# Attention scores as two 64-row matmuls side by side instead of one 128-row matmul over zero-padded queries

## The chip, the cores and the metric

The kernel runs on all eight cores of one Trainium2 chip (two dies, cores 0 to 3 and 4 to 7). Every core does the same program on its own data; no core waits for another. The metric is the device time in microseconds of the slowest core. A run can fall into a slower state, in which the cores of one die or both show a lower granted clock of TensorE (one run of control before: 2176.61 us, with 0.86 to 0.87 on cores 0 to 3 and 0.998 to 0.999 on the others, against 1933.28 us with 0.997 to 0.999 on all); such runs are left out wherever times are compared: a time given for several runs is the median of the fast ones.

"TensorE" is PE in the profile, "ScalarE" is ACT, "VectorE" is DVE, "GpSimd" is POOL.

## The reference, cut to what matters

One step of a two-layer encoder: gated linear attention (GLA), an FFN, forgetting attention (Fox), an FFN. A core has one prompt stream of 2048 tokens and four sample streams of 64 tokens with 2048 cached keys each. Only Fox changes here. It has 16 heads of 64 columns:

```python
def fox_attend(q, k, v, c_q, c_k, q_pos, k_pos):
    s = jnp.einsum('bqhd,bkhd->bhqk', q, k).astype(jnp.float32) * (FOX_HD ** -0.5)   # FOX_HD = 64
    bias = c_q.transpose(0, 2, 1)[:, :, :, None] - c_k.transpose(0, 2, 1)[:, :, None, :]
    mask = k_pos[None, :] <= q_pos[:, None]
    p = jax.nn.softmax(jnp.where(mask, s + bias, MASK_VALUE), axis=-1)
    return jnp.einsum('bqhk,bkhd->bqhd', p.astype(v.dtype), v)
# cut: projections, cumulative log-forget gates, GLA, SwiGLU FFN, RMSNorm, caches
```

## The kernel before

The kernel describes its work as nodes (a group of matmuls, an exp, a copy, a transfer). A list scheduler in Python, with a cost model of its own, fixes the order on each engine before the kernel is built; one helper emits everything, so that every instruction carries that helper's line (L566 before, L568 after). A table of seeded random changes of priority, `SHUFFLE`, was found by search against the cost model. It is tuning for one exact list of nodes.

Two heads share the 128 rows of a tile. The score matmul contracts over all 128 rows at once: the queries are stored block-diagonally, half of the buffer zero, and 512 columns (two heads by 256 queries) come out into one PSUM bank.

```python
Q = U.ring("a_q", 3, [128, 2, 2, 256], BF16)      # zeroed once; half of it stays zero
BS = Banks([0, 1, 2])                             # scores: three single banks
BO, BOS = Banks([3, 4]), Banks([5])               # outputs of prompt, of samples
BP = Banks([6, 7, 0, 1, 2])                       # projections; shares banks with the scores

def a_item(p, tt, hf, a):                         # one key block of 128 for 256 queries of two heads
    # cut
    b = BS.next()
    pt = PT.next()
    g.mm([(bank(b, 2 * w), kT[:, a * 128:(a + 1) * 128], q[:, hf, :, c0:256], True, True)], ...)
    # cut: causal mask on the diagonal
    g.act(pt[:, 0:2 * w], bank(b, 2 * w), AF.Exp, [pk(b)], [(pt.name,)], scale=0.125)
    if a == 0:
        obk[0] = BO.next()
    ob = obk[0]
    g.mm([(bank(ob, 65, ...), pt[:, ...128 columns], vt[:, a, h, :], ...) for h in range(2) for qt in range(c0 // 128, 2)], ...)

def s_item(p, s, gq):                             # samples: four cached key blocks
    b = BS.next()
    g.mm([(bank(b, 128, c0=j * 128), kc[:, ...], qb[:, s, :, :], True, True) for j in range(4)], ...)
    # cut: exp of 512 columns, four matmuls with the values
```

The softmax here doesn't subtract the row's maximum and nothing guards it: scores larger than these inputs give would overflow.

## Time and profile before

| | before |
|---|---|
| time | 1943.97 us, median of 3 runs (1942.37 to 1950.3); the profiled execution was a faster one |
| TensorE busy in the profiled run | 98% of 1931.9 us |
| Fox stage, ScalarE / VectorE / GpSimd busy | about 72% / 63% / 54% |
| granted clock of TensorE | 0.998 |

The first lines show parts 1, 3 and 4 of the page of the kernel before (its slowest core): busy us, share of the span and count of instructions for each engine; a DMA queue's packets, MB and share; the chain that ended last, by engine.

```profile
span 1931.9 us, 39044 instructions; the slowest of 8 cores (1920.0 to 1931.9 us)
...
PE 1885.6 (98%) x14130; PEld 1094.1 (57%) x14130; DVE 914.6 (47%) x1783; ACT 886.1 (46%) x1580; POOL 484.5 (25%) x573
...
q8 instruction: 118, 1.93, 0.4%
...
PE 90%; DVE 3%; issue 2%; ACT 2%; DMA 1%; POOL 1%; SPq 0%; ACTq 0%; DVEq 0%; POOLq 0%
...
```

TensorE is the limit: it is busy nearly all the time, and the chain of waits that ended last is 90% its work.

The table by stage of the same run, in three stretches of Fox (columns: stretch, its length, busy us and instructions of each engine, granted clock, share of the DMA engines, GB/s):

```profile
...
895.00:1060.00 165.00, 163.30 (x1996) 114.86 (x1994) 95.50 (x232) 121.84 (x233) 110.42 (x136) 1.00 0.76 171
1060.00:1240.00 180.00, 175.69 (x2125) 122.83 (x2123) 109.86 (x268) 129.40 (x249) 114.12 (x141) 1.00 0.74 162
1240.00:1450.00 210.00, 206.00 (x2074) 129.28 (x2072) 144.62 (x326) 146.95 (x272) 77.32 (x93) 1.00 0.46 99
...
```

No other engine is near its limit, and TensorE has 10 us of gaps in 555. The costliest exps of ScalarE on the page (out and in, count, busy us, mean ns, idle before it and what ended it):

```profile
...
L566 ACT ACTIVATE a_P_264<-ps 128x512 bf16<-128x512 f32 x96 | 57.5, 599 | 25.9 <-PE ps L566 15.5
...
L566 PE MATMUL ps<-a_q_258,a_kT_243 128*128 128x512 bf16 (+1 forms) x108 | 35.8, 366 | 0.0
...
```

An exp of 512 columns takes 0.6 us. A record of a matmul lasts 378 ns (366 on average with the narrow ones), but the next matmul starts before it ends, so what a matmul costs is the distance from its start to the next start: 216 ns for 512 columns over 128 rows, 109 ns for 256, 56 ns for 128.

### The profile page before, as it was taken

Reading aid. Unit: us, or ns where it says so; the run is one execution under the profiler, and the core shown is the slowest. Engines: PE = TensorE matmul, PEld = TensorE weight load, DVE = VectorE, ACT = ScalarE, POOL = GpSimd, SP = SyncE. Lnnn points to the kernel's source line nnn. Section 1 sums busy time; section 2 is a strip of 40 time slices with the busy share of each in tenths; the row PEclk is TensorE's granted clock in tenths of the full one; section 3 lists DMA queues with packets and bytes.
Section 4 is the critical chain, followed back from the end, with each engine's and each line's share of the span. In section 5 each row is a group of like instructions: output and inputs, shape, how many; then the busy total and the mean of one; then the engine's idle time right before and its main releaser. Section 6 shows DMA issues by size and latency. Waiting matters only on the chain.

```text
span 1931.9 us, 39044 instructions; the slowest of 8 cores (1920.0 to 1931.9 us)
## 1 busy us (share of the span) xinstructions
PE 1885.6 (98%) x14130; PEld 1094.1 (57%) x14130; DVE 914.6 (47%) x1783; ACT 886.1 (46%) x1580; POOL 484.5 (25%) x573
## 2 busy tenths in 40 slices
PE   6999999999999999999999999999999999999998
PEld 3545655455555444486776676766555555544447
DVE  3877677532111622246457566577855121162225
ACT  5776788531100611113777677776754110051112
POOL 2431111300000000017665665663213000000000
PEclk9999999999999999999999999999999999999999
DMA  9604402343244533327876876775225323495222
GB/s 187 158 8 66 103 1 47 61 74 59 45 68 80 96 67 63 62 41 174 184 170 149 169 163 140 178 163 112 56 43 90 60 45 60 82 189 108 46 45 89
DMA packets 84027, 183.69 MB, mean 95 GB/s; under 512 B 6912, under 2 KB 17024, under 8 KB 83840
## 3 DMA queue, kind: packets, MB, share of 16 engines
q0 software_dynamic: 37488, 103.88, 32.5%
q1 hardware_dynamic: 46352, 77.31, 14.2%
q8 instruction: 118, 1.93, 0.4%
q14 instruction: 69, 0.57, 0.1%
HBM read 253.96 MB, written 31.08 MB: 148 GB/s over the span
## 4 chain that ended last, share of the span: by engine, by line
PE 90%; DVE 3%; issue 2%; ACT 2%; DMA 1%; POOL 1%; SPq 0%; ACTq 0%; DVEq 0%; POOLq 0%
PE ps L566 90%; DMA gsp_out<-g_SF_111 1%; DMA x<-xin 0%; DVE x L566 0%; POOL g_rs_107 L566 0%; POOL f_rs_131 L566 0%; DVE h_3_316 L566 0%; ACT g_re_85 L566 0%; DVE h_1_142 L566 0%; DVE h_0_114 L566 0%; ACT g_Sb_84 L566 0%; ACT L566 0%; DMA g_St_125<-state_in 0%; DVE h_1_148 L566 0%; DVE h_3_306 L566 0%
## 5 line engine op out<-in xcount | busy, mean ns | idle before, releaser
L566 DVE TENSOR_TENSOR x<-ps,x 128x512 f32<-128x512 f32 (+2 forms) x344 | 200.5, 600 | 241.6 <-PE ps L566 239.3
L566 ACT ACTIVATE f_sg_300<-ps 128x512 bf16<-128x512 f32 (+1 forms) x46 | 25.8, 560 | 162.2 <-PE ps L566 147.3
L566 ACT ACT_TABLE_LOAD x45 | 57.7, 1283 | 33.7 <-PE ps L566 18.0
L566 ACT ACTIVATE a_P_264<-ps 128x512 bf16<-128x512 f32 x96 | 57.5, 599 | 25.9 <-PE ps L566 15.5
L566 DVE TENSOR_TENSOR ps<-ps,a_neg 128x256 f32<-128x256 f32 x128 | 53.2, 426 | 33.3 <-PE ps L566 32.2
L566 ACT ACTIVATE a_P_266<-ps 128x512 bf16<-128x512 f32 x96 | 57.2, 596 | 24.0 <-PE ps L566 14.6
L566 ACT ACTIVATE f_sq_190<-x 128x512 bf16<-128x512 f32 (+1 forms) x12 | 10.1, 841 | 123.9 <-PE ps L566 100.8
L566 ACT ACTIVATE a_P_262<-ps 128x512 bf16<-128x512 f32 x96 | 57.4, 598 | 19.2 <-PE ps L566 14.9
L566 ACT ACTIVATE f_sg_128<-ps 128x512 bf16<-128x512 f32 (+1 forms) x33 | 17.3, 526 | 97.1 <-PE ps L566 97.1
L566 ACT ACTIVATE a_P_265<-ps 128x512 bf16<-128x512 f32 (+1 forms) x96 | 53.2, 554 | 13.4 <-PE ps L566 10.1
L566 ACT ACTIVATE f_sq_302<-x 128x1024 bf16<-128x1024 f32 (+2 forms) x24 | 20.2, 843 | 83.3 <-DVE x L566 73.8
L566 ACT ACTIVATE a_P_263<-ps 128x512 bf16<-128x512 f32 (+1 forms) x96 | 53.5, 557 | 10.1 <-PE ps L566 7.8
L566 PE MATMUL ps<-a_oT_250,a_wo_268 128*128 128x512 bf16 (+1 forms) x160 | 56.9, 357 | 0.7 <-DVE x L566 0.5
L566 ACT ACTIVATE a_P_267<-ps 128x512 bf16<-128x512 f32 (+1 forms) x96 | 51.6, 537 | 11.8 <-PE ps L566 8.8
L566 PE MATMUL ps<-a_oT_299,a_wo_268 128*128 128x512 bf16 (+1 forms) x160 | 56.9, 357 | 0.0
L566 ACT ACTIVATE f_sq_303<-x 128x1024 bf16<-128x1024 f32 (+2 forms) x24 | 20.1, 840 | 79.9 <-DVE x L566 76.2
L566 ACT ACTIVATE f_sg_189<-ps 128x512 bf16<-128x512 f32 x22 | 13.1, 596 | 80.3 <-PE ps L566 78.0
L566 ACT ACTIVATE f_sg_301<-ps 128x512 bf16<-128x512 f32 (+1 forms) x46 | 25.7, 559 | 36.4 <-PE ps L566 36.4
L566 PE MATMUL ps<-a_q_258,a_kT_243 128*128 128x512 bf16 (+1 forms) x108 | 35.8, 366 | 0.0
L566 PE MATMUL ps<-a_q_258,a_kT_291 128*128 128x512 bf16 (+1 forms) x102 | 34.1, 368 | 0.0
L566 PE MATMUL ps<-a_q_259,a_kT_291 128*128 128x512 bf16 x100 | 32.2, 366 | 0.0
L566 ACT ACTIVATE g_re_85<-ps 128x512 f32<-128x512 f32 (+1 forms) x40 | 22.1, 551 | 20.0 <-PE ps L566 19.7
(2417 smaller groups left out, 5117.0 us busy)
## 6 DMA issues: line engine op xcount, KB each, us to landing
a_vs_292<-cv_in SPq DMA_DIRECT2D x43, 256.0 KB, 5.5
a_vs_293<-cv_in SPq DMA_DIRECT2D x43, 256.0 KB, 5.3
a_vs_298<-cv_in SPq DMA_DIRECT2D x42, 256.0 KB, 6.2
a_kc_297<-ck_in POOLq DMA_DIRECT2D x16, 512.0 KB, 8.3
a_kc_296<-ck_in POOLq DMA_DIRECT2D x16, 512.0 KB, 8.6
x<-xin SPq DMA_DIRECT2D x3, 2048.0 KB, 15.6
y_out<-x SPq DMA_DIRECT2D x6, 1024.0 KB, 9.6
f_w_143<-w_gu POOLq DMA_DIRECT2D x3, 1024.0 KB, 9.4
```

Of the source, the lines that this page charges most:

```text
L566: last = getattr(eng, m)(*[resolve(v) for v in a], **{k: resolve(v) for k, v in kw.items()})
```

## The change

The intent: with 64-row tiles TensorE is to stream head 0 on the upper half of its rows and head 1 on the lower half at the same time (an assumption before the run; in the trace of control after the two start 3 to 4 ns apart), so that no column streams over zeros and the scores cost half. The price: each change between 128-row and 64-row tiles costs TensorE time (95 ns going in and 93 ns coming out around GLA's 64-row matmuls in the trace before), so two units are coupled (`link`) and run in one stretch of the new mode; the two tiles of a pair are given different PSUM banks, so a unit owns a double bank and is made to cover two key blocks; the scores now hold four banks, which other uses lose; and all tuned order from Fox on is dropped.

```diff
-SHUFFLE = [ ... 29 entries ... ]
+SHUFFLE = [ ... 12 entries; those from Fox on dropped ... ]
+LEAD = 600.0      # ns that the first unit of a link may start before the second one's bank is free
-        Q = U.ring("a_q", 3, [128, 2, 2, 256], BF16)
+        Q = U.ring("a_q", 3, [128, 512], BF16)
-        BS = Banks([0, 1, 2])
-        BO, BOS = Banks([3, 4]), Banks([5])
+        BS = Banks([0, 2], 2, True)               # two double banks
+        BO, BOS = Banks([4]), Banks([5])
+        BP = Banks([6, 7])                        # once the first projections are done
+    def mm2(self, mms, r, w):
+        nd = self.mm(mms, r, w)
+        nd.prio -= 150
+        nd.cost = [(n, rows, True) for n, rows in nd.cost[::2]]
+        return nd
+    def link(self, a, b):
+        a.deps |= b.deps - {a.i}
+        b.deps.add(a.i)
+        a.follow, b.slave = b.i, True
+        def rows(b, c0, n, kb, q, q0):
+            return [(bank(b, n, c0=512 * h + c0), kb[64 * h:64 * h + 64, :], q[64 * h:64 * h + 64, q0:q0 + n], True, True) for h in range(2)]
-            g.mm([(bank(b, 2 * w), kT[...], q[:, hf, :, c0:256], True, True)], ...)
-            g.act(pt[:, 0:2 * w], bank(b, 2 * w), AF.Exp, ...)
+            for j in range(2):                    # two key blocks a unit
+                mms += rows(b, 256 * j, 256 - c0, kT[...], q, 256 * hf + c0)
+            return b, g.mm2(mms, ...)
+            g.act(..., bank(b, 1024)..., AF.Exp, ...)     # 1024 columns at once
+        def a_two(us):
+            qk = [a_qk(*u) for u in us]
+            if len(us) == 2:
+                g.link(qk[0][1], qk[1][1])
+            for u, (b, _) in zip(us, qk):
+                a_pv(*u, b)
 # cut: samples likewise (8 key blocks a unit, two linked units a stream), the scheduler's handling
 # of links and strict banks (strict in the second FFN too), assertions on the order, one release
 # point of the normalisation behind Fox (NAT 0.4 to 0.5), no zeroing of the query buffers
```

## The prediction

> **What bounds the kernel now.** TensorE. The page's busy line gives PE 98% of 1931.9 us, the chain of waits is 90% PE, the granted clock is 0.998 (view by core), and the idle-time view shows few waits of PE over 1 us after the first 40 us. In the Fox stage (895 to 1450 us, table by stage) PE is busy 163/165, 176/180 and 206/210 us; ACT about 72%, DVE 63%, POOL 54%. Only PE time counts there.
>
> **Removed.** A score matmul streams both heads' columns over 128 rows, half of them zeros. Start to start in the trace, 128x512 takes 216 ns, 128x256 109 ns, 128x128 56 ns. 576 prompt matmuls (64 of them 256 wide) make 117.5 us, 512 sample ones (128 wide) 28.6 us, 32 own-key ones 1.8 us: 148 us of PE. If two 64-row tiles run side by side, half goes: **-74 us**. [...] this trace has no such pair, so it is my main assumption. It is least safe for sample pairs (64 columns, about 27 ns, two weight loads in that time): 14 of the 74 us.
>
> **Added.** [...] around GLA's 64-row sample matmuls, entering costs 311-216 = 95 ns, leaving 202-109 = 93 ns, and the second matmul in each mode is 10 ns late: 208 ns a round trip. 144 prompt links of two units, 32 sample links, 8 own-key units: 184 trips, **+38 us**. Net **-36 us**.
>
> **Moved.** (1) PSUM: scores go from three single banks to two double ones, prompt outputs from two banks to one, projections from five (shared) to two. A link takes both double banks, so score, exp, exp, release becomes a loop, estimated: 0.3 us scores, 0.2 to ACT, 1.9 for two 1024-column exps (512-column ones start 0.49 us apart), 0.25 back, less 0.6 lead: 2.1 us. PE has 2.3 us of work per link in odd head pairs, 2.9 with output projections. Slack is small, and a link begun before its second bank is free can idle PE inside the mode. (2) The tuned order of Fox and the second FFN is dropped. (3) ACT falls from about 405 to 350 us, q copies halve on DVE: off the critical path. New stalls: +15 us (5 to 35).
>
> **Prediction.** 1944 - 36 + 15 = **1923 us**, range 1900 to 1950. Faster by over 2%: 0.12; within 2%: 0.82; slower by over 2%: 0.06.
>
> **Right if:** tiles of a pair start a few ns apart and the next pair 109 ns later; 184 gaps of 90 to 100 ns on each side; Fox shorter by about 20 us, GLA and the first FFN unchanged; 1024-column exps near 1.0 us; PE's waits on exps, on output normalisation or on PSUM grow from about 3 us to 10 to 30. **Wrong if:** tiles of a pair start 109 ns (samples 25 to 30 ns) apart; PE's excess between Fox matmuls doesn't grow (then faster); or the second FFN grows by over 5 us.
>
> **What would make it wrong.** Tiles that don't overlap (about 1990). [...] The exp loop, not PE, bounding the odd head pairs (about 1940). Or a schedule that hides everything and recovers the 25 us of gaps now between Fox matmuls (about 1900).

A cut marks what no trace or run of this case shows. No term of the sum is cut: 1944 - 74 + 38 + 15 = 1923 us. That two 64-row tiles run side by side, on which the -74 rests, stood as an assumption. The loop's 0.2 and 0.25 us are estimates; in the trace before, an exp that waited for a score matmul started 0.10 us after the end of its record in the median (a record lasts 0.16 us longer than the 216 ns to the next start), and a value matmul that waited for an exp started 0.14 or 0.25 us after that exp's end in most cases.

## The result, and the profile after

| | before | after |
|---|---|---|
| time, one chip | 1945.59 us (1942.37 to 1950.3, 4 runs) | 1945.69 us (1943.47 to 1952.27, 4 runs) |
| ratio | | 1.0008, 95% interval 0.9984 to 1.0032 |
| time, the chip of the first experiments (fast runs) | 1932.33 us | 1936.61 us |
| ratio | | 1.0017, 0.9992 to 1.0042 |

A ratio is the mean time of one kernel's fast runs over that of the other's in the same rounds, so it is not quite the ratio of the medians. The kernel did not become faster or slower. The forecast was 21 us less.

The page after (parts 1, 3 and 4 and two groups of part 5 of its slowest core):

```profile
span 1951.2 us, 39835 instructions; the slowest of 8 cores (1927.0 to 1951.2 us)
...
PE 1867.7 (96%) x15027; PEld 1074.7 (55%) x15250; DVE 879.8 (45%) x1679; ACT 850.3 (44%) x1228; POOL 479.3 (25%) x568
...
q8 instruction: 126, 2.06, 0.4%
...
PE 90%; issue 4%; DVE 3%; ACT 2%; DMA 1%; POOL 0%; DVEq 0%; SPq 0%; ACTq 0%; POOLq 0%
...
L568 ACT ACTIVATE a_P<-ps 128x1024 bf16<-128x1024 f32 (+1 forms) x288 | 268.3, 974 | 145.8 <-PE ps L568 125.1
...
L568 PE MATMUL ps<-a_q,a_kT 64*128 64x256 bf16 (+1 forms) x1152 | 91.2, 268 | 3.0 <-ACT a_PS L568 0.8
...
```

TensorE's busy share fell from 98% to 96%: its work shrank and its gaps grew. In the chain, "issue" (TensorE waits for nothing that the profile shows) went from 2% to 4%. Queue 8 carries 8 more packets. The exps became half as many and about 1.0 us long (the 974 ns average in narrower diagonal ones).

The first run after came from a chip on which TensorE was granted 13/16 of its clock (0.8125 in the trace) for 4 to 15 us at a time, in GLA and the first FFN too, where the change touches nothing (mean clock of a core 0.984 to 0.994). In the profiled runs on the chip of the first experiments neither kernel showed it, with the same work on all eight cores (mean clock 0.997 to 0.999 before, 0.993 to 0.998 after). The kernel before took 1942 to 1950 us on the first chip and 1932 on this one, so it was slower there too, though no trace of it from there exists. I therefore compare the two copies run on the second chip, called *control before* and *control after* below. Their view by core, before and then after:

```profile
...
core 0: 1932.2 us, clock 0.997
...
core 3: 1924.1 us, clock 0.998
...
core 7: 1923.6 us, clock 0.999
...
die 1 (median of its cores): 1926.8 us, clock 0.998
```

```profile
...
core 0: 1937.9 us, clock 0.994
...
core 4: 1937.6 us, clock 0.993
...
core 7: 1919.4 us, clock 0.998
...
die 1 (median of its cores): 1928.9 us, clock 0.996
```

After the change the best core is 4 us faster than the best before, and the worst is 6 us slower than the worst before. The cores of this run spread over 18.5 us instead of 8.6 (7.7 to 18.5 in the four runs of the change there, 8.6 to 10.7 in the fast runs of before). The metric takes the worst.

The table by stage of control after, its slowest core, answers to the one of before:

```profile
...
895.00:1060.00 165.00, 154.77 (x2421) 106.21 (x2420) 81.46 (x198) 114.40 (x123) 114.30 (x142) 0.98 0.83 177
1060.00:1240.00 180.00, 167.13 (x2427) 111.31 (x2427) 99.41 (x231) 110.38 (x119) 108.19 (x135) 0.98 0.76 157
1240.00:1450.00 210.00, 195.61 (x2358) 118.57 (x2355) 132.52 (x287) 135.44 (x154) 74.91 (x89) 0.99 0.41 88
...
```

TensorE now has 37 us outside its matmul records in 555, and ScalarE has 38 us less to do. The stages say where the time is: from the start of Fox's projections to the last output projection, the mean core (of six, see below) takes 569.5 us before and 566.4 after; everything behind that takes 487.3 before and 492.3 after; everything ahead of it is equal (870.5 us).

### Where the gain went

From the starts of all TensorE matmuls in the trace I split the time from Fox's projections to the end. "Columns" is what the same matmuls take when each follows the last without a stall. A "mode change" is 95 ns at each switch between 128-row and 64-row tiles, as measured in GLA before. What is left is excess: waits where the program has a semaphore wait, outside the links and inside them; gaps where it has none; and matmuls at half clock. Mean us per core:

| | before | after | difference | forecast |
|---|---|---|---|---|
| columns | 1027.7 | 959.8 | -67.9 | -74 |
| mode changes | 0 | 35.3 | +35.3 | +38 |
| semaphore waits outside links | 18.0 | 27.8 | +9.8 | |
| semaphore waits inside links | 0 | 10.8 | +10.8 | |
| gaps without a semaphore wait | 3.6 | 13.3 | +9.7 | |
| half clock | 0.8 | 4.1 | +3.3 | |
| small remainders | 3.5 | 4.2 | +0.7 | |
| stalls, the last five together | 25.9 | 60.2 | **+34.3** | **+15** |
| sum | 1053.6 | 1055.3 | +1.7 | -21 |

(Six of the eight cores, those whose matmul records are complete; their mean end moved from 1927.4 to 1929.2 us. The time of the second matmul in a stretch, about 10 ns late, counts in columns here and under mode changes in the forecast, so read the first two lines together: -33 against -36.)

So the main assumption held, and the mode change was costed well. The gain was lost to stalls, more than twice as many as forecast. The kernel's own cost model could have warned: built again afterwards, it gives 1900.7 us for the kernel before and 1897.0 for the change, 4 us less and not 21. A stretch of starts in the trace of control after, core 5, shows all of it (start in ns, distance to the one before, columns x rows):

```
996385    60  130x128  sample values      998502    32   65x128  prompt values
996537   152  256x64   scores, head 0     998626   124  256x64   scores, head 0
996540     3  256x64   scores, head 1     998630     4  256x64   scores, head 1
996656   116  256x64   head 0, block 2    998745   115  256x64   head 0, block 2
996660     4  256x64   head 1             998749     4  256x64   head 1
996765   105  256x64   second unit        999113   364  256x64   second unit
996769     4  256x64                      999119     6  256x64
996875   106  256x64                      999221   102  128x64
996878     3  256x64                      999239    18  128x64
997080   202  130x128  sample values      999387   148   65x128  prompt values
```

The tiles of a pair start 3 to 4 ns apart. Going in costs 152 - 60 = 92 ns, coming out 202 - 106 = 96. The left link runs through. In the right one the second unit starts 364 ns after the pair before it instead of about 110: it waits 250 ns for its double bank, inside the mode. The timeline view of the same two links shows it as lengths (start, length, group):

```profile
...
996.54 0.61 PE L568 MATMUL ps<-a_q,a_kT 64*128 64x256 bf16 x8
...
998.63 0.83 PE L568 MATMUL ps<-a_q,a_kT 64*128 64x256 bf16 x8
...
```

The view of TensorE's waits in Fox (what it waited for, us in total, times, longest), of control before and then control after, the fastest core of each kernel:

```profile
...
PE ps L566 <- ACT a_P L566: 2.8, 6, 0.7
PE ps L566 <- issue: 2.0, 2, 1.3
PE ps L566 <- DVE x L566: 0.7, 4, 0.2
...
```

```profile
...
PE ps L568 <- issue: 8.7, 10, 1.7
PE ps L568 <- ACT a_P L568: 4.7, 10, 2.2
PE ps L568 <- DVE x L568: 4.1, 10, 0.6
PE ps L568 <- DVE a_stg L568: 2.1, 5, 0.8
PE ps L568 <- DVE a_rl L568: 1.3, 2, 0.8
...
```

Each of these lists sums a few long waits. "ACT a_P" is a score or value matmul waiting for an exp, "DVE x" an output projection waiting for a PSUM bank, "DVE a_stg" a projection waiting for one, "DVE a_rl" the single bank of outputs. These were all expected. "issue" was not: the longest such gap, on core 0 of control after:

```profile
...
967.16 0.67 PE L568 MATMUL ps<-a_vt,a_P 128*128 128x65 bf16 x16
972.29 1.89 PE L568 MATMUL ps<-h,a_wqk 128*128 128x512 bf16 x4 [4.45 <-issue]
...
```

No semaphore stands ahead of the matmul at 972.29. What the trace does show is the DMA queue that carries TensorE's own instructions, queue 8. Its 126 packets have 16,384 bytes each, 2.06 MB, and this fits: 2 x 15,250 matmuls and weight loads and 1,733 semaphore instructions are 32.2 thousand, which makes 64 bytes for one and 256 for a packet. (The other instruction queue, 14, has 61 packets and 0.50 MB, which fits the 7.8 thousand instructions of the other engines.) Around this gap, on core 0, the packets (start and end, us) were

```
950.34 to 951.65     955.42 to 957.39     969.87 to 970.75     980.65 to 981.60
```

The third came 12.5 us after the end of the second, and TensorE went on 1.54 us after it had landed. All of the gaps over 0.3 us without a semaphore wait in Fox behave so: in control after 50 of them on six cores, and every one ends 1.25 to 1.62 us after the end of such a packet, while packets are about 9 us apart. The count of instructions says the same: in every one of these gaps, in control before too, TensorE stops after 443 of its instructions plus a whole multiple of 256. I read this as TensorE running out of instructions. A packet starts at the earliest some 296 instructions before such a place in the count (why 40 more than the 256 of a packet is not shown). The four matmuls behind the gap, 400 to 427 ns apart instead of 216, then ran at half clock (the traces of before and after have stretches of granted clock 0.5, most often 3.4 us long). Half clock is the next item of the table: on this core it came five times in Fox, each around the end of a gap of 2.4 to 4.6 us: four times one without a semaphore wait, once a semaphore wait of 2.4 us.

These gaps took 3.6 us per core before and 13.3 us after.

### The profile page after: what moved, and what is told of

The parts are those of the page before. It is cut to its first block, busy times and chain, and to the rows that moved or that the text cites. A ratio compares the mean times of both kernels' runs of the same rounds, so it can differ in the third digit from the quotient of the medians.

```text
span 1951.2 us, 39835 instructions; the slowest of 8 cores (1927.0 to 1951.2 us)
## 1 busy us (share of the span) xinstructions
PE 1867.7 (96%) x15027; PEld 1074.7 (55%) x15250; DVE 879.8 (45%) x1679; ACT 850.3 (44%) x1228; POOL 479.3 (25%) x568
## 3 DMA queue, kind: packets, MB, share of 16 engines
q8 instruction: 126, 2.06, 0.4%
HBM read 253.96 MB, written 31.08 MB: 146 GB/s over the span
## 4 chain that ended last, share of the span: by engine, by line
PE 90%; issue 4%; DVE 3%; ACT 2%; DMA 1%; POOL 0%; DVEq 0%; SPq 0%; ACTq 0%; POOLq 0%
PE ps L568 90%; DVE h L568 1%; DVE x L568 1%; ACT a_P L568 1%; DMA x<-xin 0%; DMA a_vs<-cv_in 0%; ACT f_sq L568 0%; DVE a_stg L568 0%; ACT L568 0%; DVE ps L568 0%; ACT a_PS L568 0%; ACT g_sq L568 0%; ACT f_rs L568 0%; ACT g_re L568 0%; ACT g_Sb L568 0%
## 5 line engine op out<-in xcount | busy, mean ns | idle before, releaser
L568 PE MATMUL ps<-h,f_w 128*128 128x512 bf16 (+1 forms) x2070 | 388.5, 346 | 5.6 <-DVE f_a L568 1.9
L568 ACT ACTIVATE a_P<-ps 128x1024 bf16<-128x1024 f32 (+1 forms) x288 | 268.3, 974 | 145.8 <-PE ps L568 125.1
L568 DVE TENSOR_TENSOR f_a<-ps,f_sg 128x512 bf16<-128x512 f32 (+1 forms) x202 | 129.0, 640 | 434.2 <-PE ps L568 424.2
L568 PE MATMUL ps<-h,f_v 128*128 128x512 bf16 x1380 | 309.6, 384 | 1.6
L568 PEld LDWEIGHTS ps<-h,f_w 128*128 128x128 bf16 x2112 | 207.0, 99 | 178.9 <-issue 14.8
L568 PEld LDWEIGHTS ps<-h,f_v 128*128 128x128 bf16 x1408 | 139.3, 99 | 170.8 <-issue 20.6
L568 PE MATMUL ps<-f_a,f_d 128*128 128x512 bf16 (+1 forms) x1039 | 190.2, 343 | 0.9
L568 PE MATMUL ps<-f_a,f_e 128*128 128x256 bf16 (+2 forms) x1224 | 155.4, 287 | 0.6
L568 POOL TENSOR_TENSOR a_v<-a_vs,a_wexp 128x512 bf16<-128x512 f32 x128 | 134.2, 1058 | 67.2 <-DMA a_vs<-cv_in 39.9
L568 PE MATMUL ps<-h,a_wqk 128*128 128x512 bf16 (+1 forms) x590 | 134.1, 361 | 14.1 <-issue 10.7
L568 DVE SCALAR_TENSOR_TENSOR h<-x,cst,f_rs 128x512 bf16<-128x512 f32 (+1 forms) x128 | 80.0, 695 | 11.0 <-ACT f_rs L568 10.8
## 6 DMA issues: line engine op xcount, KB each, us to landing
f_v<-w_gu POOLq DMA_DIRECT2D x22, 1024.0 KB, 10.2
```

Of the source, the lines that this page charges most:

```text
L568: last = getattr(eng, m)(*[resolve(v) for v in a], **{k: resolve(v) for k, v in kw.items()})
```

## The experiments

There were three questions. Is the loss the dropped order, the new structure's waits (the loop of two double banks, the banks taken from others), or the supply of instructions? Every kernel was correct unless I say that it was wrong. "Before" in a ratio is always the kernel before, in the same rounds on the same chip. All differences are under 2%; I call one a difference where its interval leaves out 1. The traces come from four chips; the stages ahead of Fox took 870 to 871 us (mean core) in all whose order there is the same, so I compare them. "Waits" below are semaphore waits of TensorE outside links / inside links, "fetch gaps" those without a semaphore wait, mean us per core, as in the table above.

### The two kernels again, side by side

No edit.

> Control: the kernel before, unchanged, profiled on the same chip as the other three. Every theory expects 1940 to 1950 us; its trace shows whether the 13/16 clock episodes in the first GLA and FFN stages of the profile after belong to the chip (then they are here too, some 3 us before Fox) or to the change.

> Control: the changed kernel, unchanged, on the same chip. Expected ratio to the kernel before 0.998 to 1.003. Between the start of the Fox projections and the end the accounting of the trace should give again about 67 us fewer columns than before, about 39 us of mode changes, 11 us of waits between the two units of a link and 20 us of other new gaps.

The copy of before took 1933.28 us (fast run, below the 1940 to 1950 expected; another slow, at 2176.6). The copy of the change took 1936.61 against 1932.33 us, ratio 1.0017 (0.9992 to 1.0042). The result is reproduced on another chip, without the 13/16 clock.

### What the lost tuning is worth to the kernel before

```diff
-SHUFFLE = [ ... 29 entries ... ]
+SHUFFLE = [ ... the 12 entries of the changed kernel ... ]
```

> The kernel before with only the shuffles of issue order that the changed kernel kept (12 of 29; the 17 of Fox and of the FFNs dropped). Theory structure (the gain was eaten by fewer PSUM banks and by waiting for the second bank of a link): at most 5 us slower than before. Rival theory lost tuning (the gain was eaten because the tuned order was dropped): 15 to 30 us slower than before, with 15 to 30 us of new gaps between matmuls in Fox.

1937.72 us, ratio 1.0028 (1.0008 to 1.0047): about 5 us. Waits 23.6 against 18.0. Losing its tuning costs the kernel *before* little, and all of it in Fox (576.4 us instead of 569.5; 487.6 behind it). The 5 us that the change loses behind Fox therefore need not come from the dropped entries: the strict banks of the second FFN and the moved release point changed too, and no run took them apart. That did not settle what the missing tuning costs the *changed* kernel, as the last experiments show.

### The tiles of a pair set apart in program order

```diff
 def mm2(self, mms, r, w):
     # cut
+    nd.ins = nd.ins[::2] + nd.ins[1::2]     # both blocks of head 0, then both of head 1
```

> The changed kernel with each unit's score matmuls issued as all of head one, then all of head two, in the same overall order of instructions: [...] a prompt unit takes about 3 x 109 ns instead of 2 x 109, a sample unit about 15 x 27 ns instead of 8 x 33. That is about 38 us more of TensorE time. If TensorE is the bound in Fox: 25 to 40 us slower than the changed kernel. If the loop score, exp, exp, release is the bound: less than 15 us slower, and the waits inside links shrink by several us. If tiles never overlapped: no change.

1937.76 us, ratio 1.0029 (1.001 to 1.0049). My premise failed. I meant to take the overlap away, and the estimate of 38 us supposes that this order does so, which no trace had shown. But in a prompt unit the four starts lay at 0, 7, 120 and 127 ns, and the next unit began at 230. Strictly in program order, with the rows of one head busy some 107 ns for each of its matmuls, the four would start at about 0, 107, 111 and 218 ns (an estimate from the 109 ns cadence). So tiles of different rows still ran side by side; which of the two middle matmuls went first, the trace does not name. Only in sample units, where eight of one head precede eight of the other, was some of it lost (740 ns from a link's first start to the first matmul behind it, instead of 573): with small losses elsewhere about 6 us more of columns, where I had expected 38. The time hardly differs from that of control after, because fetch gaps fell from 13.3 to 9.3 us and waits in links from 10.8 to 8.9. The engine spent longer on the same instructions, and the stalls gave it back. This was a first hint that the density of instructions matters.

### More semaphore instructions in the kernel before

```diff
             for dn in nd.waits:
                 eng.wait_ge(sems[dn.pos[0]], dn.tick)
+                # cut: `again` keeps the semaphore and value of TensorE's last wait
+            for _ in range(nd.extra):        # 3 ahead of each score group: a wait already satisfied
+                eng.wait_ge(*again)
```

> The kernel before, same order of work, with three waits that are already satisfied put ahead of each score group of 1 to 4 matmuls in Fox: 2112 more TensorE instructions of 64 bytes, 8 more 16-KB packets on the instruction queue, about as many as the change adds (1950). Theory fetch (TensorE runs out of fetched instructions where they are dense; in the profiles so far all 119 long gaps without a semaphore wait end 1.0 to 1.6 us after such a packet): those gaps grow from about 3.5 us per core in Fox to 8 or more, and the time by 4 to 10 us. Rival (the long gaps come with the tile mode or the changed order, not with the number of instructions): they stay at 3 to 5 us and the time within 3 us.

1967.01 against 1933.25 us, ratio 1.0174 (1.0155 to 1.0193). The waits themselves cost about 16 ns each on TensorE, 34 us in all, so the instructions became only half as much denser in time as in the change (TensorE's median time for 296 of them is 11.4 us before, 10.6 here and 9.8 in the change). Fetch gaps were 3.0 us, no more than before. A greater number of instructions is thus no cause by itself; whether density is one, this run cannot say.

### A smaller lead inside a link

```diff
-LEAD = 600.0
+LEAD = 350.0
```

> The changed kernel with the lead of a link's first unit over its second bank cut from 600 to 350 ns (the first unit takes about 320 ns with the mode change). Waits inside links fall from 10.8 us per core to under 4. If they are plain loss: 5 to 8 us faster than the changed kernel. If the loop of scores and exps sets the pace, the same time shows up as waits elsewhere: within 3 us of it.

1941.11 us, ratio 1.0037 (1.0015 to 1.006). Waits inside links fell from 10.8 to only 8.2 us (under 4 was expected), and those outside rose from 27.8 to 36.2. This fits a loop of score, exp and release that sets its pace wherever one waits, but does not show it: the scheduler placed everything anew, and the waits outside rose by more than those inside fell.

### Banks shared again

```diff
-        BO, BOS = Banks([4]), Banks([5])
+        BO, BOS = Banks([4]), Banks([5, 6, 7])
-        BP = Banks([6, 7])
+        BP = Banks([5, 6, 7])
```

> The changed kernel with projections and sample outputs sharing three PSUM banks instead of two and one. If too few banks for the projections cause the new semaphore waits outside links (28 us per core against 18 before), these fall by 5 to 10 us and the time by 4 to 8 us. If they come from elsewhere (exps, output bank of the prompt part): no change beyond 2 us.

1930.13 us, ratio 0.9981 (0.9961 to 1.0001). Fox did not become shorter (572.7 us), but what lies behind it fell from 492.3 to 483.2. The waits outside links, which were to fall by 5 to 10 us, fell by about 1. The order had changed as well, since the scheduler places everything anew, so the run settles nothing.

### Sample scores as before, prompt scores in 64-row tiles

```diff
-            nd = [g.mm2([m for j in range(8) for m in rows(b, j * 64, 64, kc[...], qb, s * 64)], ...) for gq, b in enumerate(bs)]
-            g.link(*nd)
+            for gq, b in enumerate(bs):          # qb zero-padded again
+                nd = g.mm([(bank(b, 128, c0=j * 128), kc[...], qb[:, s, :, :], True, True) for j in range(8)], ...)
+                nd.prio -= 150
```

> The changed kernel with the sample scores back in one 128-row matmul for both heads (zero-filled queries), in the same double banks and without links; the prompt part stays tiled. TensorE columns grow by about 12 us, 40 of 184 mode round trips (8 us) and 1088 instructions go, waits inside links fall by about 4 us. If instruction fetch was part of the loss, gaps without a semaphore wait fall from about 13 us per core to 8 or less and the kernel is 3 to 8 us faster than the changed one; if not, it is within 2 us.

1926.14 us, ratio 0.9957 (0.9937 to 0.9977). By columns and mode changes it should lose 4.8 us (columns +12.4, mode changes -7.6). Instead the mean core gains 12 (1929.2 to 1917.3): waits inside links 5.9, fetch gaps 4.4. The pairs of 64 columns put two matmuls and two weight loads into 30 ns. Taking them out makes the stream of instructions sparser (TensorE's time for 296 instructions, median: 10.5 us instead of 9.8), and the fetch gaps shrink to a third. The order changed here too, so this is not density alone.

### Half the exp

Each exp takes half its columns; the order of TensorE, VectorE and ScalarE stays that of the change (the cost model is told the full size). Its output is wrong, which doesn't matter for the time. Relative error 0.19.

```diff
-g.act(..., [:, :, 0:w], AF.Exp, ...)
+g.act(..., [:, :, 0:w // 2], AF.Exp, ...).cost = 50 + 2 * w / 1.2     # and the sample exps likewise
# cut: what the exps leave out is set to one at the start
```

> Wrong results on purpose: the changed kernel with the same order of instructions on TensorE, each exp of Fox reading and writing only half of its columns (the rest of its tile is set to one at the start), so an exp takes about 0.5 us instead of 1.0. If the loop of scores and exps through two double banks makes the waits inside links and the waits of value products and scores on ACT, the waits inside links fall from 10.8 us per core to under 3, other semaphore waits from 28 to under 22, and the time by 10 to 20 us. If banks released by VectorE (projections, output sums) and fetch make the loss, the time falls by less than 5 us.

1918.11 against 1930.49 us, ratio 0.9939 (0.9922 to 0.9955). Waits inside links fell from 10.8 to 1.2 us, so these are the loop over exp; waits outside stayed at 28.2; fetch gaps fell to 6.2, which nobody had expected and which is not explained (see the last experiment). The wait view of core 7 (control after is above):

```profile
...
PE ps L568 <- issue: 6.9, 7, 2.8
PE ps L568 <- DVE x L568: 4.6, 10, 0.6
...
PE ps L568 <- ACT a_P L568: 0.7, 1, 0.7
...
```

"ACT a_P" went from 4.7 to 0.7 us, while "DVE x", the banks of the projections, stayed. Half of what I expected did not come: I had thought that most of the other waits were behind exps too.

### A new search, in three kernels

The random changes of priority were searched again with the kernel's own cost model, some 11 thousand trials for each kernel, and only for what comes after GLA: for the change with shared banks, for that with sample scores as before as well, and for the kernel before. (In the first two one transfer of the prompt's forget gates got a semaphore of its own, since a new order made a shared one unsafe.)

```diff
-SHUFFLE = [ ... 12 entries ... ]
+SHUFFLE = [ ... 377, 288 and 86 entries ... ]
-LEAD = 600.0
+LEAD = 400.0            # 550 in the second
```

> The changed kernel, projections and sample outputs on three shared banks, and the issue order of everything after GLA searched anew with the kernel's own cost model (11 thousand trials; lead 400 ns). Theory (the gain was not lost for good: about 29 us of net TensorE time stay available, the order only has to fit the fewer banks): semaphore waits, inside links and outside, fall from 39 us to under 20, fetch gaps stay at 10 to 13 us, time 15 to 30 us below the kernel before. Rival (structure: two double banks cannot feed this density): at most 8 us below.

> The same search on the version with sample scores on 128 rows (11 thousand trials; lead 550 ns). Its columns are 12 us more and its mode changes 8 us fewer than with all scores tiled, and the dense runs of 64-column pairs are gone: fetch gaps at 4 to 6 us per core. Time 20 to 33 us below the kernel before, and within 5 us of the other searched version, below it if fetch costs as much as in the unsearched pair.

> Control for the two searches: the kernel before with its order searched for as many trials from its own tuned start. If searching by itself explains the gain of the other two, it gains as much; expected 2 to 6 us below the kernel before, because its waits (18 us per core) are already few.

| | time, us | ratio | waits | fetch gaps |
|---|---|---|---|---|
| change, shared banks, searched | 1906.98 | **0.9884** (0.9867 to 0.99) | 10.2 / 6.1 | 9.0 |
| the same, sample scores as before | 1915.22 | 0.9916 (0.9896 to 0.9936) | 12.1 / 0.9 | 11.2 |
| before, searched | 1932.56 | 1.0013 (0.9998 to 1.0028) | 14.5 / 0 | 3.4 |

The first beats both kernels, by 1.2%. The second was to be within 5 us of it, with fetch gaps of 4 to 6; it is 6 us slower by the ratios, with 11. The search gives nothing to the kernel before: its cost model saw 4.7 us there, the chip none. The wait view of the best, core 7:

```profile
...
PE ps L664 <- issue: 6.2, 8, 1.1
PE ps L664 <- ACT a_P L664: 2.8, 5, 1.2
...
PE ps L664 <- DVE x L664: 0.5, 1, 0.5
...
```

"DVE x" went from 4.1 us in control after to 0.5, "issue" only from 8.7 to 6.2.

### The order alone

The runs so far had changed banks and order together, so I searched the change as it is.

```diff
-SHUFFLE = [ ... 12 entries ... ]
+SHUFFLE = [ ... 377 entries ... ]
-LEAD = 600.0
+LEAD = 450.0
```

> The change as it is, with its bank split untouched, and only the order of instructions searched anew (random priority entries from Fox on, tried against the kernel's own cost model, LEAD 450). Theory O (a good part of the new stalls is the order that was dropped, and the new structure merely answers to a search): the cost model says 22 us less, so ratio 0.988 to 0.993; the semaphore waits outside links fall from 28 us to under 18, and the second FFN shrinks from 492 us to about 470 to 485. Rival S (the split of the PSUM banks sets those waits, so that the 21 us of the re-searched kernel with shared banks came from sharing): ratio 0.997 or more and waits outside links of 24 us or more. In both the instruction gaps stay at 8 to 14 us.

1916.12 against 1931.03 us, ratio 0.9922 (0.9906 to 0.9938): 15 us below the kernel before, some 18 below the change. Waits fell to 16.2 / 5.1, what lies behind Fox from 492.3 to 478.9 us, fetch gaps stayed at 11.5. The cost model had promised 22 us against the change. The wait view, core 7:

```profile
...
PE ps L664 <- issue: 10.9, 9, 2.5
PE ps L664 <- DVE x L664: 1.5, 2, 1.0
...
PE ps L664 <- ACT a_P L664: 1.1, 4, 0.5
...
```

So with the split of the banks untouched, an order fitted to the new structure (and a smaller lead, which alone had gained nothing) removes 17 of the 21 us of new semaphore waits. This shows that the order can remove them, not that the dropped entries had caused them: the new ones are 365 more, found by a search of their own. The kernel with shared banks is some 7 us faster still, but from another search, so that this is not the banks' alone.

### Less traffic beside the instructions

Wrong in the sample outputs: from the second head pair on, only half of each cached key and value block is loaded. (The comparison with the reference still passed.) On TensorE, ScalarE and VectorE the order of instructions is exactly that of the change.

```diff
-g.dma("pool", kc[:], ck_d[p, s], ...)
+kn = SEQ if p == 0 else SEQ // 2
+g.dma("pool", kc[:, 0:kn], ck_d[p, s, :, 0:kn], ...).nbytes = 128 * SEQ * 4    # the scheduler sees the full size
# and the values likewise: two of four key blocks in each transfer
```

> The change with half of every cached key and value block loaded from the second head pair on (wrong on purpose in the sample outputs; the rest of the tile keeps older numbers). Order, instruction count and TensorE's work are those of the change; only the cache traffic in Fox falls, 50 MB to about 27 MB per core. Theory F (the packets of TensorE's instructions come late because they share the DMA engines with the cache loads): gaps without a semaphore wait fall from 13 us per core to under 6, half-clock loss with them, and the ratio to 0.994 to 0.998. Rival D (the packets' own latency against the denser instructions is enough): gaps stay at 9 to 15 us and the ratio within 0.002 of the 1.0017 of the change.

Ratio 0.995 (0.9932 to 0.9968), fast runs near 1921 us. The two tables by stage, core 7 of control after and then of this kernel:

```profile
...
880.00:970.00 90.00, 86.75 (x1342) 61.29 (x1339) 41.27 (x98) 56.58 (x63) 71.25 (x91) 1.00 0.87 206
970.00:1060.00 90.00, 87.07 (x1363) 58.01 (x1360) 54.38 (x127) 67.07 (x72) 57.76 (x70) 1.00 0.75 167
1060.00:1240.00 180.00, 170.41 (x2543) 114.81 (x2541) 98.99 (x232) 115.72 (x125) 113.54 (x141) 1.00 0.75 161
...
```

```profile
...
880.00:970.00 90.00, 88.19 (x1357) 62.45 (x1355) 42.71 (x100) 56.56 (x63) 71.11 (x91) 1.00 0.69 167
970.00:1060.00 90.00, 87.07 (x1365) 58.08 (x1362) 54.25 (x127) 67.02 (x72) 56.89 (x70) 1.00 0.44 104
1060.00:1240.00 180.00, 171.69 (x2554) 115.52 (x2550) 99.17 (x232) 116.10 (x125) 111.45 (x141) 0.99 0.49 111
...
```

The share of the DMA engines fell from 0.75 to 0.44 and 0.49, and from 0.87 to 0.69 while the first pair still loads all. HBM reads fell from 253.96 to 224.60 MB in the whole run. Fetch gaps fell from 13.3 to 2.3 us per core (8 gaps on six cores instead of 50), Fox from 566.4 to 552.7 us. Everything else stayed: waits 26.8 / 10.8, columns 959.3, what lies behind Fox 492.4. A packet's start came a median 4.3 us after the earliest point in TensorE's count where packets start, instead of 5.6. So without the full traffic of the cache loads the instruction packets are not late enough to matter. The rival, the packets' own latency and the density alone, is refuted as a sufficient cause. Density still decides how late is too late: before and after the change the packets' lag is alike (median 5.3 us in control before and 5.6 in control after, 8.5 at the 90th percentile in both), but TensorE's time for 296 instructions, the most that it has left when a packet starts, is 11.4 us in the median before and 9.8 after, 10.2 and 8.2 us at the 10th percentile.

Traffic and density are not the whole of it. With half the exp the order on TensorE is that of the change, its instructions are as dense (9.4 us for 296), and the DMA engines are as busy (0.77 from 970 to 1240 us, against 0.76, mean of six cores), yet the packets' median lag was 4.6 us and the fetch gaps halved. When the packets meet the cache loads may matter too; no run isolates it.

## Why the prediction was wrong, point by point

- **"Removed: -74 us" was right**, with its main assumption: -68 us, of which some 3 us is the late second matmul of each stretch, booked elsewhere in the forecast. Pairs of 64 columns, the part called least safe, overlap too (30 ns a pair instead of 56).
- **"Added: +38 us" was right**: 35 us at 95 ns a switch, plus those 3.
- **"Net -36 us" was nearly right**: -33.
- **"New stalls: +15 us (5 to 35)" is the step that failed.** Two of its causes were named and a third was missed, and its size was wrong: it measured +34, at the upper end of its own range (+10 semaphore waits outside links, +11 inside, +10 instruction fetch, +3 half clock). The central forecast then stood 20 us too low, with a chance of 0.82 for "within 2%", which is what came.
  - The exp loop was named, and the half-exp run confirms it: about 10 us inside links. The slack of a link was put at 0.2 to 0.8 us from *averages* of work per link. A wait comes from the single link whose exps are late; averages hide that.
  - The order was named, with no figure. It was the largest part that could be removed: searched anew, the same change is 18 us faster, against the 5 us that the kernel before loses with its tuning. The tuning of the old kernel is no measure of what the new one needs.
  - Instruction fetch was not thought of: +10 us, and part of the +3 us of half clock. The signs were on the page of before: a queue called instruction with 118 packets, "issue" the largest of TensorE's waits in Fox (5.9 us on the core of that page), DMA engines three quarters busy there.
- **The signs.** "Tiles of a pair start a few ns apart, next 109": right (3 to 4, then 105 to 109). "Fox shorter by about 20 us": wrong, 3 us. "GLA and the first FFN unchanged": right. "1024-column exps near 1.0 us": right, 1.02 in the full ones. "TensorE's waits grow from 3 to 10 to 30 us": right, but it left out those that wait on nothing. "Or the second FFN grows by over 5 us" was listed as a sign of being wrong; it grew by 5.0, and the order search takes back 13.
- **The clock.** Measured was half clock of 4.1 us per core after against 0.8 before, and on the core looked at it came with long gaps.

What stays open: the search changes many waits at once, so no single order can be named as the bad one. The kernel with sample scores as before, shared banks and a new order still has 11 us of fetch gaps although its stream is sparser, and half the exp lost half of them at the same density; when the cache loads come may matter, but no run took that apart. And the run with half the caches let the scheduler keep its old plan, so a kernel that truly needed fewer transfers would also be ordered differently.

## What to carry to other kernels

When work is taken from a busy engine, book the stalls by running the schedule again for the new structure before judging the structure: here the same change was worth 0 us against the kernel before in an inherited order and 15 us in a searched one (22 with shared banks), while the old kernel gained nothing from the same search. Packing more and smaller instructions into the time of fewer raises the demand for instructions themselves (here TensorE's time for 296 of them fell from 11.4 to 9.8 us, and fetch gaps rose from 3.6 to 13.3 us per core); look at the instruction queue, and at gaps that no semaphore explains, in a stage in which the DMA engines are already busy (a share of 0.75 here). Forecast waits in a loop from its tightest pass, not from its mean.
